# Rolling a matrix by 100 columns: head loads moved from GpSimd's ring to those of SP and ACT, in stages of 256 rows on 64 partitions

## The chip, the core and the metric

The kernel runs on one core of one Trainium2 chip. The metric is the device time of one execution in microseconds (us). The core has 16 DMA engines, which serve several rings (queues): one that the SP engine (SyncE) issues into, one for ACT (ScalarE), and one for POOL (GpSimd), which is a ring written by software. VectorE (DVE) does the only computing, if copying within the on-chip memory (SBUF) may be called that.

## The reference

```python
def setup_inputs():
    return {"x": np.random.randn(8192, 8192).astype(np.float32), "shift": 100}

def reference(x, shift):
    return np.roll(x, shift, axis=1)
```

Every row of 8192 floats (32 KB) is shifted right by 100 places: `out[r, c] = x[r, c - 100]`, and the last 100 floats of a row of x become the first 100 of that row of out. The matrix is 268.44 MB, read once and written once. There is no arithmetic.

## The kernel before

With a shift of s = 100, a is 100 rounded up to a multiple of 128, that is 128, and then made 256 by lines 21 and 22; g = a - s = 156. The output is cut at column a.

**The copies** (lines 34 to 43) write columns 256 to 8191 of out straight from columns 156 to 8091 of x, HBM to HBM. Rows go in 128 blocks of 64. A block is four DMAs (j = 0 to 3) of 16 rows each, four rows apart: 16 pieces of 31,744 bytes, 496 KB. DMAs with j even go to SP, those with j odd to ACT. In the last four blocks each is cut at a middle column into two of 15,872 bytes a row. These are 528 DMAs and 260.08 MB. The framework puts a semaphore wait on a copy, so that SP and ACT issue a new one when an earlier one has landed.

**The heads** (lines 60 to 80) are the first 256 columns of out. They go through SBUF, in 16 stages of 512 rows: 128 partitions with four neighbouring rows (Q = 4) in each. For each stage GpSimd issues three loads:

- line 72 loads t, three pieces of 256 floats (1 KB) per partition: the last 100 floats of one row and the first 156 of the next lie side by side in x, so one piece holds the head of one row and the rest of the head of the next
- line 73 loads into h the 100 floats (400 bytes) that end the fourth row
- line 76 loads into h the 156 floats (624 bytes) that begin the first row

DVE then copies the two parts of t to their places in h (lines 74 and 77). All 16 stages have their own t and h, so no load waits for a buffer. The stores come in a second loop (lines 79 and 80), also on GpSimd: one DMA per stage, which writes 512 pieces of 1 KB to out. GpSimd issues in the order of the program: 48 loads, then 16 stores.

Copies and heads touch different columns of out, and nothing orders them against each other, apart from the engines that they share.

Of the kernel before, what the change touches and what calls it, by code (L numbers as in the profile page):

```python
# [1 line left out]

# [4 lines left out]


@with_exitstack
def kernel(  # L10
    ctx: ExitStack,
    tc: tile.TileContext,
    x: bass.AP,
    shift: int,
    out: bass.AP,
):
    nc = tc.nc
    n_rows, n_cols = x.shape
    s = shift % n_cols
    a = -(-s // 128) * 128  # L20
    if 0 < a <= 384 and a + 128 <= n_cols:
        a += 128
    g = a - s
    P = nc.NUM_PARTITIONS
    engines = [nc.sync, nc.scalar]
    n_chunks = 16
    rows = n_rows // n_chunks

    xm = x.rearrange("(c e j) w -> c j e w", e=16, j=4)
    om = out.rearrange("(c e j) w -> c j e w", e=16, j=4)
    if a < n_cols:
        blocks = n_rows // 64
        mid = (a + n_cols) // 256 * 128
        for c in range(blocks):
            parts = ((a, mid), (mid, n_cols)) if c >= blocks - 4 and a < mid else ((a, n_cols),)  # L40
            for j in range(4):
                for lo, hi in parts:
                    engines[j % 2].dma_start(out=om[c, j, :, lo:hi], in_=xm[c, j, :, lo - s:hi - s])
    if a == 0:
        return


    if a > 512:
        for i in range(n_chunks):
            r = slice(i * rows, (i + 1) * rows)  # L50
            nc.gpsimd.dma_start(out=out[r, :s], in_=x[r, n_cols - s:])
            if g > 0:
                nc.gpsimd.dma_start(out=out[r, s:a], in_=x[r, :g])
        return

    Q = 4  # L60
    n_st = n_rows // (P * Q)
    reads = ctx.enter_context(tc.tile_pool(name="reads", bufs=n_st))
    heads = ctx.enter_context(tc.tile_pool(name="heads", bufs=n_st))
    xt = x.rearrange("(k p q) c -> k p q c", q=Q, p=P)
    ot = out.rearrange("(k p q) c -> k p q c", q=Q, p=P)
    tiles = []
    for k in range(n_st):
        t = reads.tile([P, Q - 1, a], x.dtype)
        h = heads.tile([P, Q, a], x.dtype)
        lead = bass.AP(tensor=x.tensor, offset=(k * P * Q + 1) * n_cols - s,  # L70
                       ap=[[Q * n_cols, P], [n_cols, Q - 1], [1, a]])
        nc.gpsimd.dma_start(out=t[:], in_=lead)  # L72
        nc.gpsimd.dma_start(out=h[:, Q - 1, :s], in_=xt[k, :, Q - 1, n_cols - s:])  # L73
        nc.vector.tensor_copy(h[:, :Q - 1, :s], t[:, :, :s])  # L74
        if g > 0:
            nc.gpsimd.dma_start(out=h[:, 0, s:], in_=xt[k, :, 0, :g])  # L76
            nc.vector.tensor_copy(h[:, 1:, s:], t[:, :, s:])  # L77
        tiles.append(h)
    for k, h in enumerate(tiles):
        nc.gpsimd.dma_start(out=ot[k, :, :, :a], in_=h[:])  # L80


# [1 line left out]
_INS = ['x', 'shift']  # L84
_OUTS = [((8192, 8192), 'float32')]

_NUMBERS = {'shift': 100}


# [26 lines left out]
```

## Time and profile before

| what | value |
|---|---|
| time of the runs, median of 3 | 826.37 us (825.38 to 826.65) |
| span of the profiled execution, first to last instruction | 828.0 us |
| DVE busy | 12.3 us, 32 instructions |
| POOL busy (issuing included) | 41.3 us, 68 instructions |
| copies: time from issue to landing, median | 12.7 us (halves 5.9 to 6.0) |
| stores of heads, issue to landing, median | 108.2 us |
| loads of heads, issue to landing, median | 50.6 us (t), 43.2 and 49.9 us (the two into h) |
| first and last issue of a head load | 1.3 and 241.7 us |
| first and last issue of a head store | 242.2 and 379.6 us |
| chain that ended last | DMA 29% of the span by name, 15% a queue that it can't name |

The profiled execution has no separate time besides its span; the span is 1.6 us above the median of the runs.

The page's slices cut the span into 40 parts of 20.7 us. "DMA" there is the mean busy share of the 16 DMA engines in tenths, "GB/s" what these moved; a copy from HBM to HBM counts its bytes once. A row of a DMA queue has packets, MB, and the time of its packets as a share of 16 engines' span; q1 and q10 are the rings of SP and ACT, q0 is GpSimd's. A window's table does the same for a part of the span. A row of waits has the waiting engine and line, what it waited for, the total in us, how often, and the longest. A row of DMA issues has what was moved, the issuing engine (SPq, ACTq, POOLq), how many, KB each, and the median us from issue to landing.

### The profile page before, as it was taken

What the parts mean: (1) busy time and instruction counts of PE and PEld (TensorE: products, weight loads), DVE (VectorE), ACT (ScalarE), POOL (GpSimd) and SP (SyncE); (2) the same over time, 40 slices, a digit from 0 to 9 for tenths busy, and PEclk for the clock granted to TensorE, in tenths of its full rate; (3) what the DMA queues carried; (4) which work ended last, traced back from release to release, by engine and by line L of the source; (5) the groups of instructions that cost most, each with busy time, mean ns of one, the idle gap of its engine ahead of it and who ended that gap; (6) DMA issues with size and microseconds to landing.
All of it is one profiled execution on the core that took longest, in us unless ns stands there. A gap on an engine that the chain in (4) does not pass through costs nothing. (4 is left out here: it accounts for less than half of the span.)

```text
span 828.0 us, 689 instructions
## 1 busy us (share of the span) xinstructions
DVE 12.3 (1%) x32; POOL 41.3 (5%) x68
## 2 busy tenths in 40 slices
DVE  0000000000010000000000000000000000000000
POOL 2011000000021100000000000000000000000000
DMA  9999999999999999999999999999999999999998
GB/s 308 340 350 334 344 340 337 337 339 344 337 342 348 352 351 345 354 339 346 347 341 344 333 325 325 319 330 333 330 324 322 335 330 328 322 331 328 327 314 300
DMA packets 22278, 276.90 MB, mean 334 GB/s; under 512 B 9473, under 2 KB 9729, under 8 KB 13825
## 3 DMA queue, kind: packets, MB, share of 16 engines
q1 hardware_dynamic: 8448, 130.04, 46.1%
q10 hardware_dynamic: 8448, 130.04, 44.7%
q0 software_dynamic: 5376, 16.78, 8.4%
q14 instruction: 6, 0.04, 0.0%
HBM read 268.44 MB, written 268.44 MB: 648 GB/s over the span
## 5 line engine op out<-in xcount | busy, mean ns | idle before, releaser
L80 POOL DMA_DIRECT2D out_dram<-h x16 | 11.5, 724 | 126.6 <-DMA out_dram<-h 86.8
L76 POOL DMA_DIRECT2D h<-in_x_dram x16 | 8.7, 542 | 141.4 <-DMA t<-in_x_dram 141.4
L72 POOL DMA_DIRECT2D t<-in_x_dram x16 | 12.2, 762 | 30.8 <-DMA h<-in_x_dram 30.0
L73 POOL DMA_DIRECT2D h<-in_x_dram x16 | 8.9, 559 | 39.9 <-DMA h<-in_x_dram 39.9
L74 DVE COPY h<-t 128x300 f32<-128x300 f32 x16 | 6.1, 382 | 260.2 <-DMA t<-in_x_dram 260.2
L77 DVE COPY h<-t 128x468 f32<-128x468 f32 x16 | 7.5, 467 | 0.0
L97 POOL MEMSET const-float32-0.0<- 128x1 f32 x1 | 0.1, 99 | 0.2 <-issue 0.2
L97 POOL MEMSET const-bfloat16-1.0<- 128x1 bf16 x1 | 0.1, 102 | 0.0
L97 POOL MEMSET const-float32-1.0<- 128x1 f32 x1 | 0.1, 99 | 0.0
L97 POOL MEMSET const-uint8-127<- 128x1 uint8 x1 | 0.1, 99 | 0.0
## 6 DMA issues: line engine op xcount, KB each, us to landing
out_dram<-in_x_dram ACTq DMA_DIRECT2D x248, 496.0 KB, 12.7
out_dram<-in_x_dram SPq DMA_DIRECT2D x248, 496.0 KB, 12.7
out_dram<-h POOLq DMA_DIRECT2D x16, 512.0 KB, 108.2
t<-in_x_dram POOLq DMA_DIRECT2D x16, 384.0 KB, 50.6
out_dram<-in_x_dram SPq DMA_DIRECT2D x16, 248.0 KB, 6.0
out_dram<-in_x_dram ACTq DMA_DIRECT2D x16, 248.0 KB, 5.9
h<-in_x_dram POOLq DMA_DIRECT2D x16, 78.0 KB, 43.2
h<-in_x_dram POOLq DMA_DIRECT2D x16, 50.0 KB, 49.9
```

Of the source, the lines that this page charges most:

```text
L72: nc.gpsimd.dma_start(out=t[:], in_=lead)
L73: nc.gpsimd.dma_start(out=h[:, Q - 1, :s], in_=xt[k, :, Q - 1, n_cols - s:])
L74: nc.vector.tensor_copy(h[:, :Q - 1, :s], t[:, :, :s])
L76: nc.gpsimd.dma_start(out=h[:, 0, s:], in_=xt[k, :, 0, :g])
L77: nc.vector.tensor_copy(h[:, 1:, s:], t[:, :, s:])
L80: nc.gpsimd.dma_start(out=ot[k, :, :, :a], in_=h[:])
L97: nc = _bacc.Bacc("TRN2", target_bir_lowering=False, num_devices=1)
```

## The change

The 16 stages of 512 rows on 128 partitions become 32 stages of 256 rows on 64 partitions (H = 64), four rows in each partition as before. The three loads of a stage are issued by SP and ACT: t by the one, the two loads into h by the other, and the roles alternate from stage to stage. They are placed among the copies: after every second block of copies (step = 128 // 64 = 2) comes one stage, so that the stages follow blocks 1, 3, 5, up to 63, and blocks 64 to 127 have none. The buffers are fewer: 4 for t and 12 for h, used in turn. The store of a stage stays with GpSimd, and follows directly on its stage in program order. DVE's copies are the same with half the partitions, 64 of them in place of 32. The copies have the same shapes, order and engines.

```diff
+    blocks = n_rows // 64
+    mid = (a + n_cols) // 256 * 128
+
+    def copies(c):
+
+        last = None
+        parts = ((a, mid), (mid, n_cols)) if c >= blocks - 4 and a < mid else ((a, n_cols),)
+        for j in range(4):
+            for lo, hi in parts:
+                if lo < hi:
+                    last = engines[j % 2].dma_start(out=om[c, j, :, lo:hi], in_=xm[c, j, :, lo - s:hi - s])
+        return last
...
     Q = 4
-    n_st = n_rows // (P * Q)
-    reads = ctx.enter_context(tc.tile_pool(name="reads", bufs=n_st))
-    heads = ctx.enter_context(tc.tile_pool(name="heads", bufs=n_st))
-    xt = x.rearrange("(k p q) c -> k p q c", q=Q, p=P)
-    ot = out.rearrange("(k p q) c -> k p q c", q=Q, p=P)
-    tiles = []
-    for k in range(n_st):
-        t = reads.tile([P, Q - 1, a], x.dtype)
-        h = heads.tile([P, Q, a], x.dtype)
-        lead = bass.AP(tensor=x.tensor, offset=(k * P * Q + 1) * n_cols - s,
-                       ap=[[Q * n_cols, P], [n_cols, Q - 1], [1, a]])
-        nc.gpsimd.dma_start(out=t[:], in_=lead)
-        nc.gpsimd.dma_start(out=h[:, Q - 1, :s], in_=xt[k, :, Q - 1, n_cols - s:])
+    H = P // 2
+    n_st = n_rows // (H * Q)
+    xt = x.rearrange("(k p q) c -> k p q c", q=Q, p=H)
+    ot = out.rearrange("(k p q) c -> k p q c", q=Q, p=H)
+    reads = ctx.enter_context(tc.tile_pool(name="reads", bufs=4))
+    heads = ctx.enter_context(tc.tile_pool(name="heads", bufs=12))
+    step = max(1, blocks // (2 * n_st))
+    for c in range(blocks):
+        copies(c)
+        k, at = divmod(c, step)
+        if at != step - 1 or k >= n_st:
+            continue
+        t = reads.tile([H, Q - 1, a], x.dtype)
+        h = heads.tile([H, Q, a], x.dtype)
+        lead = bass.AP(tensor=x.tensor, offset=(k * H * Q + 1) * n_cols - s,
+                       ap=[[Q * n_cols, H], [n_cols, Q - 1], [1, a]])
+        one, other = engines[k % 2], engines[1 - k % 2]
+        one.dma_start(out=t[:], in_=lead)
+        other.dma_start(out=h[:, Q - 1, :s], in_=xt[k, :, Q - 1, n_cols - s:])
         nc.vector.tensor_copy(h[:, :Q - 1, :s], t[:, :, :s])
         if g > 0:
-            nc.gpsimd.dma_start(out=h[:, 0, s:], in_=xt[k, :, 0, :g])
+            other.dma_start(out=h[:, 0, s:], in_=xt[k, :, 0, :g])
             nc.vector.tensor_copy(h[:, 1:, s:], t[:, :, s:])
-        tiles.append(h)
-    for k, h in enumerate(tiles):
         nc.gpsimd.dma_start(out=ot[k, :, :, :a], in_=h[:])
```

More of the change, by code (lines that the diff above doesn't have):

```diff
@@ L35 @@
     om = out.rearrange("(c e j) w -> c j e w", e=16, j=4)
-    if a < n_cols:
-        blocks = n_rows // 64
-        mid = (a + n_cols) // 256 * 128
-        for c in range(blocks):
[L40 to L49, printed above, removed]
+    blocks = n_rows // 64
[8 more added lines that the diff above has]
+        return last
+    if a == 0 or a > 512:
+        for c in range(blocks):
+            copies(c)
+        for i in range(n_chunks if a else 0):
             r = slice(i * rows, (i + 1) * rows)
@@ L60 @@
     Q = 4
-    n_st = n_rows // (P * Q)
-    reads = ctx.enter_context(tc.tile_pool(name="reads", bufs=n_st))
-    heads = ctx.enter_context(tc.tile_pool(name="heads", bufs=n_st))
-    xt = x.rearrange("(k p q) c -> k p q c", q=Q, p=P)
-    ot = out.rearrange("(k p q) c -> k p q c", q=Q, p=P)
-    tiles = []
-    for k in range(n_st):
-        t = reads.tile([P, Q - 1, a], x.dtype)
-        h = heads.tile([P, Q, a], x.dtype)
-        lead = bass.AP(tensor=x.tensor, offset=(k * P * Q + 1) * n_cols - s,
-                       ap=[[Q * n_cols, P], [n_cols, Q - 1], [1, a]])
-        nc.gpsimd.dma_start(out=t[:], in_=lead)
-        nc.gpsimd.dma_start(out=h[:, Q - 1, :s], in_=xt[k, :, Q - 1, n_cols - s:])
+    H = P // 2
[6 more added lines that the diff above has]
+    for c in range(blocks):
+        copies(c)
+        k, at = divmod(c, step)
[8 more added lines that the diff above has]
+        other.dma_start(out=h[:, Q - 1, :s], in_=xt[k, :, Q - 1, n_cols - s:])
         nc.vector.tensor_copy(h[:, :Q - 1, :s], t[:, :, :s])
         if g > 0:
-            nc.gpsimd.dma_start(out=h[:, 0, s:], in_=xt[k, :, 0, :g])
+            other.dma_start(out=h[:, 0, s:], in_=xt[k, :, 0, :g])
             nc.vector.tensor_copy(h[:, 1:, s:], t[:, :, s:])
-        tiles.append(h)
-    for k, h in enumerate(tiles):
         nc.gpsimd.dma_start(out=ot[k, :, :, :a], in_=h[:])
```

## The prediction

> **What bounds the kernel now.** I read the page's slices and DMA queues first, because the engines hardly compute.
>
> ```profile
> DMA  9999999999999999999999999999999999999998
> GB/s 308 340 350 334 344 340 337 337 339 344 337 342 348 352 351 345 354 339 346 347 341 344 333 325 325 319 330 333 330 324 322 335 330 328 322 331 328 327 314 300
> ...
> q1 hardware_dynamic: 8448, 130.04, 46.1%
> q10 hardware_dynamic: 8448, 130.04, 44.7%
> q0 software_dynamic: 5376, 16.78, 8.4%
> ...
> HBM read 268.44 MB, written 268.44 MB: 648 GB/s over the span
> ```
>
> The 16 DMA engines have no idle slice. q1 and q10 are the rings of SP and ACT with the copies, q0 is GpSimd's ring with the heads. The second half, where heads are gone, runs at a lower GB/s, so the rate has to be read by stage. The same table for three windows follows: 20 to 240 us (copies and head loads), 280 to 460 us (copies and head stores), 500 to 790 us (copies alone); columns are packets, MB, share of the 16 engines.
>
> ```profile
> q10 hardware_dynamic: 2129, 33.88, 42.1%
> q1 hardware_dynamic: 2146, 33.91, 40.2%
> q0 software_dynamic: 2579, 7.04, 17.1%
> ```
>
> ```profile
> q1 hardware_dynamic: 1747, 27.75, 46.8%
> q10 hardware_dynamic: 1746, 27.72, 43.4%
> q0 software_dynamic: 1887, 6.87, 10.6%
> ```
>
> ```profile
> q1 hardware_dynamic: 3001, 47.69, 50.9%
> q10 hardware_dynamic: 2997, 47.46, 48.5%
> ```
>
> A copy reads and writes HBM, so its bytes count twice there; a head load or store counts once. Copies alone: 95.15 MB in 290 us are 328.1 GB/s, 656 in HBM traffic. With loads: copies 67.79 MB in 220 us are 308.1, loads 32.0, together 648. With stores: copies 55.47 MB in 180 us are 308.2, stores 38.2, together 655. The HBM sum is the same within 1.3% in all three, although q0 took 17.1% of the engines' time in one and nothing in another. So HBM traffic sets the pace, and the engines' busy time stretches to fill the span: in the load window a copy ran at 308.1/16/0.823 = 23.4 bytes per ns of engine time, alone at 20.6. The change moves no byte less.
>
> **What the heads cost now.** Loads: 220 x (1 - 308.1/328.1) = 13.4 us for 7.04 MB, so 16.0 us for all 8.39 MB. Stores, the same way: 10.9 us for 6.87 MB, 13.3 us in all. The copies' 260.08 MB at 328.1 GB/s take 792.7 us; the sum is 822.0, and 6.0 us of the 828.0 us span are start and end. The profiled span is 1.6 us above the median of the runs shown (826.37), so I subtract 1.6 at the end.
>
> **Loads on the rings of SP and ACT.** The floor is HBM alone: 8.39 MB at 656 GB/s are 12.8 us, a gain of 3.2 us. The other end of the hidden case is today's 16.0, no gain. Nearest row between: the stores, whose equal bytes cost 13.3. I take the middle, 14.6: **-1.4 us**. This holds only while HBM stays the bound. In engine time the loads took 0.171 x 220 x 16 = 602 us for 7.04 MB in 2579 packets, 11.7 bytes per ns, 233 ns per packet. On q0 pieces of rows are merged: 16 stages of 640 loaded and 512 stored pieces (1 KB or less) are 18,432 pieces, in 5376 packets, landing marks among them. On q1 and q10 a copy has 32 packets for 16 pieces, one per piece and one mark, and no row shows a hardware piece under 15.5 KB. So each stage may now be 20 small packets per engine (12 + 4 + 4), 640 in all. By bytes they cost 8.39 MB/16/11.7 = 45 us per engine, 70 ns a packet, as now; by packets, 640 x 233 = 149 us. Room: the first 64 blocks and all heads take about 130.04 MB/328.1 + 16.0 + 13.3 = 426 us; copies at 23.4 bytes per ns need 347 us of each engine, stores (305 us of engine time for 6.87 MB, 22.5 bytes per ns) 23 us. That leaves 56 us, 87 ns a packet. I take the bytes' price, because the pieces and their sources stay the same; the packets' price goes into the range.
>
> The Trainium skill, "DMA: Bandwidth & Descriptors", speaks against the change: "Rules for kernel authors" wants 128 partitions and at least 1 MiB per DMA, and "Anatomy of one DMA" gives about 2.0 us fixed for each. By that, 48 more transfers would be an estimate of 96 us if none were covered; the trace lets today's 48 land after 43 to 51 us each without such a sum. Its section "Issuing engines are not separate DMA queues" says that another issuer saves only issue time; by that my -1.4 would be 0.
>
> **Fewer copies in flight.** The queue's own waits and the issue rows:
>
> ```profile
> SPq L43 <- DMA out_dram<-in_x_dram: 680.3, 260, 4.9
> ```
>
> ```profile
> out_dram<-in_x_dram ACTq DMA_DIRECT2D x248, 496.0 KB, 12.7
> out_dram<-in_x_dram SPq DMA_DIRECT2D x248, 496.0 KB, 12.7
> out_dram<-h POOLq DMA_DIRECT2D x16, 512.0 KB, 108.2
> ```
>
> SP waits 680 of 828 us for its earlier copies. 528 copies of 12.7 us in 828 us are 8.1 in flight: a copy is issued when the one eight before it has landed. If that limit counts the loads too, 3 of 11 places go to them, so 5.8 copies on average, 5 at worst. The end of the run shows a shallower ring: there the eight in flight are halves (248 KB), worth four copies. The table of windows (length, DVE, POOL, clock, DMA share, GB/s):
>
> ```profile
> 801.00:822.00 21.00, 0.00 (x0) 0.00 (x0) 1.00 0.94 321
> 806.00:824.00 18.00, 0.00 (x0) 0.00 (x0) 1.00 0.96 330
> ...
> 500.00:800.00 300.00, 0.00 (x0) 0.00 (x0) 1.00 0.99 328
> ```
>
> At a depth of four the rate is 2.1% lower or 0.6% higher, by where the window is cut. 5.8 lies 0.55 of the way from eight to four: 0.55 x 426 us x these ends gives +4.9 to -1.4 us. I take the middle, **+1.7 us**.
>
> **Issue and compute, at nothing.** The 96 added issues, 48 on each of SP and ACT, cost 0.51 to 0.86 us each (the copies' shortest and longest rows), 24 to 41 us per engine; SP's 680 us of waiting hide them. Without that cover a copy behind would be late by up to three issues, 2.6 us, less than the 7.7 us that five copies last (508 KB at 328 GB/s are 1.55 us). POOL loses 48 issues (12.2 + 8.9 + 8.7 us) and has 32 stores at up to 0.72 us. DVE's 64 copies at 0.38 to 0.47 us are 24 to 30 us, where 12.3 were, on an engine at 1%.
>
> **New waits.** A load into t waits for DVE's copies four stages back, one into h for the store twelve stages back; behind either stand that ring's copies, and behind those the end. A stage is eight copies and its heads: 426/32 = 13.3 us, so the waits fall due 53 and 160 us later. Stores on q0 were issued one per landing every 13.8 us from 283.4 to 379.6 us (seven steps), 6.9 us for half the size: the ring is half loaded, and its longest landing, eight deep, was 119.3 us. So I cost it at 0. In the other case, each us past 160 is a us on one ring while the other still feeds the engines, so less than that us on the end.
>
> **Sum.** 828.0 - 1.4 + 1.7 = 828.3, less 1.6: **826.7 us**. What the measurement can tell from no change is about 0.2%, 1.65 us: same is 824.7 to 828.0.
>
> **Rivals.**
> *Loads at HBM's price and the depth free: faster.* 828.0 - 3.2 - 1.6 = 823.2, with the depth's good end (-1.4) 821.8. For it: the load window's 648 against 656, and the 330 of one window at a depth of four. Against: a longer line of small packets ahead of copies.
> *The engines become the bound: slower.* Place: the first 426 us, where 20 small packets per stage and engine stand in line with the copies. It decides from 87 ns a packet on; today's price by bytes is 70, by packets 233. At 110 ns: 640 x 110 = 70 us, 14 over the room, 828.3 + 14 - 1.6 = 841. At the geometric middle, 128 ns, 82 us: 853. The far end, 149 us, gives 920. For it: no row shows hardware packets this small. Against: bytes, pieces and sources are those of today.
> *The shallow ring starves the engines: slower.* 4.9 us with loads at 16.0: 828.0 + 4.9 - 1.6 = 831.3. For it: the share 0.94 at the end. Against: the 330 beside it.
> *It doesn't do what it says:* if most of the ring's time went on as before, nothing changes, which is inside the forecast.
>
> **Chances.** Forecast (824.5 to 829.5) 0.45, of it 0.04 faster, 0.21 same, 0.20 slower; HBM price 0.30, faster; engines 0.16 and starving 0.09, slower. So faster 0.34, same 0.21, slower 0.45. The range is 820 to 842: about 0.05 lies below, in gains that no row prices, and 0.1 above, in the engines' case past 110 ns.
>
> **What would show it.** Right: q0 with 8.39 MB of stores alone; HBM sums of 648 to 656 in every window; time to landing of a copy in the first half near 5.8 x 1.6 = 9 us; loads taking near 45 us of engine time; no wait of SP or ACT for a store. Wrong: HBM sums under 640 in the first half, idle shares there, or small packets over 87 ns each. The prediction falls if the first half's HBM rate moves by over 1%, or if the second half's differs at all.

## The result, and the profile after

The changed kernel is slower by half a per cent: 830.93 us median of 13 runs (825.99 to 833.75), where the kernel before had 826.37 us (825.26 to 829.17) beside it. The ratio is 1.005, with a 95% interval of 1.0036 to 1.0064, so 3.0 to 5.3 us were lost. The forecast was 826.7 us in a range of 820 to 842, with slower as the likeliest class at 0.45. So the time lies in the range, but outside the forecast's own band of 824.5 to 829.5.

The profiled execution after spans 828.5 us and took 830.3 us, so 1.8 us lie around the span. The other kernels of this study have 1.7 to 2.0 us there too. If that holds for the profile of the kernel before, its 828.0 us span belongs to an execution of about 829.8 us, 3.4 us above its median. So the two profiles lie only 0.5 us apart where the medians lie 4.6 us apart, and the small loss can't be read off the two spans. It takes pairs of timed runs.

The page's slices and DMA queues after:

```profile
DMA  9999999999999999999999999999999999999998
GB/s 308 341 352 346 340 354 338 331 339 353 334 330 325 363 339 346 351 338 353 329 358 333 326 326 328 334 333 326 326 330 328 320 326 330 323 334 336 328 307 304
...
q1 hardware_dynamic: 14336, 134.24, 48.9%
q10 hardware_dynamic: 14336, 134.24, 47.3%
q0 software_dynamic: 2560, 8.39, 2.5%
...
HBM read 268.44 MB, written 268.44 MB: 648 GB/s over the span
```

The change did what it says: q0 holds the stores' 8.39 MB alone, and q1 and q10 got 4.2 MB each. Their packets went from 8448 to 14,336. Of these 5888, 5120 are pieces of head loads (320 per engine and ring, 640 for both, one packet for every piece), and the rest are landing marks. The engines are as full as before.

The DMA issues of the first 426 us (count, KB each, median us to landing), in which all the loads lie:

```profile
out_dram<-in_x_dram ACTq DMA_DIRECT2D x128, 496.0 KB, 9.3
out_dram<-in_x_dram SPq DMA_DIRECT2D x128, 496.0 KB, 9.1
out_dram<-h POOLq DMA_DIRECT2D x31, 256.0 KB, 9.6
t<-in_x_dram SPq DMA_DIRECT2D x16, 192.0 KB, 12.0
t<-in_x_dram ACTq DMA_DIRECT2D x16, 192.0 KB, 12.4
```

A copy lands after 9.1 to 9.3 us, where the median of the kernel before was 12.7: fewer copies are in flight (256 of some 9.2 us in 426 us are 5.5 on average, where the prediction worked out 8.1 for the kernel before), as they would be if loads hold places among the eight transfers that SP and ACT have under way together. Stores land after 9.6 us, where eight deep they took 108.2. The longest rows of SP's own waits:

```profile
SPq L41 <- DMA out_dram<-in_x_dram: 511.8, 194, 6.2
SPq L73 <- DMA out_dram<-in_x_dram: 63.9, 16, 6.3
SPq L41 <- DMA t<-in_x_dram: 50.7, 16, 5.8
SPq L41 <- DMA h<-in_x_dram: 6.5, 12, 1.1
```

Line 41 is the copy, lines 72, 73 and 76 are the three loads. Loads wait for copies and copies for loads, as places come free. No row of SP names a store, so the buffers of t and h did not hold up its ring. The view has no rows for ACT; that ACT did not wait either is concluded from the stores, which land after 9.6 us, where a buffer of h is needed again only some 160 us later.

### The profile page after: what moved, and what is told of

It is laid out like the page before. It is cut to its first block, busy times and chain, and to the rows that moved or that the text cites. A ratio compares the mean times of both kernels' runs of the same rounds, so it can differ in the third digit from the quotient of the medians.

```text
span 828.5 us, 913 instructions
## 1 busy us (share of the span) xinstructions
DVE 23.8 (3%) x64; POOL 18.9 (2%) x36
## 3 DMA queue, kind: packets, MB, share of 16 engines
q0 software_dynamic: 2560, 8.39, 2.5%
## 4 chain that ended last, share of the span: by engine, by line
DMA 51%; issue 1%; SPq 1%; ACTq 0%; DVE 0%; POOLq 0%; DVEq 0%
DMA out_dram<-in_x_dram 36%; DMA h<-in_x_dram 8%; DMA t<-in_x_dram 7%; SPq L41 1%; ACTq L41 0%; POOLq L109 0%; DVE h L74 0%; DVE h L77 0%; DVEq L74 0%; POOLq L78 0%; SPq L72 0%; SPq L73 0%; ACTq L73 0%
## 5 line engine op out<-in xcount | busy, mean ns | idle before, releaser
L78 POOL DMA_DIRECT2D out_dram<-h x32 | 18.7, 584 | 417.4 <-DVE h L77 417.4
L74 DVE COPY h<-t 64x300 f32<-64x300 f32 x32 | 11.5, 359 | 411.9 <-DMA t<-in_x_dram 354.6
L77 DVE COPY h<-t 64x468 f32<-64x468 f32 x32 | 14.7, 459 | 0.0
## 6 DMA issues: line engine op xcount, KB each, us to landing
t<-in_x_dram ACTq DMA_DIRECT2D x16, 192.0 KB, 12.4
```

## The experiments

Two theories stood at the start. "Depth" says that the loads take places from the copies. "Packets" says that the 20 small packets per engine and stage cost more than HBM's price. A "place" is one of the eight transfers under way together; "HBM's price" is bytes over 656 GB/s, and the "HBM sum" of a window counts the bytes of copies twice and those of heads once. The first four runs take the kernel apart. All times below are medians, beside runs of the kernel before on the same chip (826.7 to 827.2 us). A bracket has the ratio to these and its 95% interval. The ratio is not always that of the two medians, so small steps are also given by it.

### The copies alone

Both pools, the stage's body and its condition are cut from the changed kernel.

```diff
     for c in range(blocks):
         copies(c)
-        k, at = divmod(c, step)
...
-        nc.gpsimd.dma_start(out=ot[k, :, :, :a], in_=h[:])
```

> Leaves out the heads altogether: columns 0 to 255 of out are not written, only the 528 copies run. The window rates priced the heads of the kernel before at 16.0 + 13.3 us, so all theories expect 826.4 - 29.3 = about 797 us. It is the base line for the next three runs. If it is above 805, the heads were hidden more than the windows say; below 790, they cost more.

Measured: 798.89 us (ratio 0.9655, 0.9642 to 0.9668). The heads of the kernel before, 826.89 us beside this run, cost 28.0 us in all, where HBM's price for 16.78 MB at 656 GB/s is 25.6. So it had only some 2.4 us to give.

### Tiny loads in the loads' places

```diff
+        t = reads.tile([16, 3, 16], x.dtype)
         one, other = engines[k % 2], engines[1 - k % 2]
-        one.dma_start(out=t[:], in_=lead)
...
+        one.dma_start(out=t[:, 0], in_=xm[c, 0, :, :16])
+        other.dma_start(out=t[:, 1], in_=xm[c, 1, :, :16])
+        other.dma_start(out=t[:, 2], in_=xm[c, 2, :, :16])
```

> Leaves out the heads as copies_only does, but issues three tiny loads (16 pieces of 64 bytes) on SP and ACT after every second block, at the places where the changed kernel has its head loads. They take the same places in the line of eight DMAs in flight, with hardly any bytes and 3 small packets per engine in place of 20. Theory 'depth' (the loads take 3 of 11 places, so fewer copies are in flight): 3 to 5 us above copies_only, and a rate below 325 GB/s in the first 400 us. Theory 'packets' (the 20 small packets per engine empty the HBM for a moment): within 1 us of copies_only.

Measured: 800.45 us (0.9668, 0.9652 to 0.9683), 1.6 us above the copies alone, with intervals that overlap. That lies between what "packets" (within 1 us) and "depth" (3 to 5 us) had said. DMA issues from 20 to 240 us:

```profile
out_dram<-in_x_dram SPq DMA_DIRECT2D x71, 496.0 KB, 8.3
out_dram<-in_x_dram ACTq DMA_DIRECT2D x70, 496.0 KB, 8.4
t<-in_x_dram ACTq DMA_DIRECT2D x27, 1.0 KB, 9.9
t<-in_x_dram SPq DMA_DIRECT2D x26, 1.0 KB, 9.6
```

A tiny load holds its place for nearly 10 us, about as long as a real one (6.6 to 12.4 us in the changed kernel), presumably because it stands in its ring behind copies. Copies land after 8.3 us, so 141 in 220 us are 5.4 in flight, as few as in the changed kernel, and still only about a third of the loss is seen. The rate did not fall below 325 GB/s, as "depth" asked; it was 327.

### The loads alone, on SP and ACT and on GpSimd

From the changed kernel, and from the kernel before, DVE's copies and the stores are cut.

```diff
-        nc.vector.tensor_copy(h[:, :Q - 1, :s], t[:, :, :s])
...
-            nc.vector.tensor_copy(h[:, 1:, s:], t[:, :, s:])
...
-        nc.gpsimd.dma_start(out=ot[k, :, :, :a], in_=h[:])
```

> Leaves out DVE's copies and the head stores: the copies and the head loads of the changed kernel on SP and ACT, nothing else. Theory 'depth': copies_only + 12.8 (HBM's price of 8.39 MB) + 3 to 5 = about +17 us, and the difference to tiny_loads is 12.8. Theory 'packets': +17 to +21 us too, but the difference to tiny_loads is 16 or more. Theory 'neither' (the loads are as cheap as HBM allows and the loss lies in the stores or their order): +13 us.

> Leaves out DVE's copies and the head stores of the kernel before: its copies and its 48 head loads on GpSimd's ring. The windows priced these loads at 16.0 us, so copies_only + 16. If the change lost its time in the loads, this is 3 to 5 us below loads_hw; if they are equal, the time was lost elsewhere.

Measured: 817.96 us on SP and ACT (0.9888, 0.9874 to 0.9901), 814.56 us on GpSimd (0.9849, 0.9835 to 0.9862). Over the copies alone the loads cost 19.1 us there and 15.7 us here. The gap of 3.4 us (0.39% by the ratios) is most of the change's loss, though intervals of 0.13% on either side leave some 1 to 5.5 us open. The two runs differ in the ring and also in the stage size, 64 against 128 partitions, so the gap can't be put down to the ring alone. The difference to the tiny loads is 17.5 us, where "depth" expected 12.8 and "packets" 16 or more. DVE's copies and the stores add 13.0 us to the one (830.93, from the first pair of runs) and 12.3 to the other (826.89).

The DMA queues from 20 to 240 us (packets, MB, share), first the copies alone, then with loads on SP and ACT, then with loads on GpSimd:

```profile
q10 hardware_dynamic: 2272, 35.88, 50.7%
q1 hardware_dynamic: 2286, 36.26, 49.4%
```

```profile
q1 hardware_dynamic: 5282, 36.64, 49.5%
q10 hardware_dynamic: 5327, 36.87, 49.2%
```

```profile
q1 hardware_dynamic: 2140, 33.97, 40.9%
q10 hardware_dynamic: 2134, 33.88, 39.5%
q0 software_dynamic: 2842, 7.73, 19.3%
```

Alone, copies move 72.14 MB, 656 GB/s of HBM traffic. With loads on SP and ACT, 17 stages of 0.262 MB were issued there, 4.46 MB, so copies had 69.05 MB: 2 x 313.9 + 20.3 = 648 GB/s. With loads on GpSimd it is 2 x 308.4 + 35.1 = 652 GB/s, although these windows hold 1.7 times the loads. So GpSimd's loads, in stages of 128 partitions, lowered the HBM sum less than those on SP and ACT in stages of 64, although they took more engine time.

### Fewer and longer packets

```diff
         lead = bass.AP(tensor=x.tensor, offset=(k * H * Q + 1) * n_cols - s,
-                       ap=[[Q * n_cols, H], [n_cols, Q - 1], [1, a]])
+                       ap=[[Q * n_cols, H], [1, (Q - 1) * a]])
...
-        one.dma_start(out=t[:], in_=lead)
+        one.dma_start(out=t[:].rearrange("p q c -> p (q c)"), in_=lead)
```

> Leaves out DVE's copies and the head stores like loads_hw, and loads t as one piece of 3 KB per partition (768 floats in a row of x, not the three row ends) in place of three of 1 KB. The same three DMAs per stage, places, bytes and order; 12 packets per engine and stage in place of 20. Measured before: copies alone 798.9, with tiny loads 800.45, loads_hw 817.96, loads_sw 814.56. Of loads_hw's 19.1 us, 12.8 are HBM's price and 1.6 the places; 4.7 are left. Theory 'packets' (the number of small packets costs them): 8 of 20 packets less save 1.9 to 4.7, so 813 to 816. Theory 'depth' or 'order': no change, 818.

Measured: 815.24 us (0.9875, 0.9854 to 0.9895) against 817.96 (0.9888, 0.9874 to 0.9901). By the medians the step is 2.7 us, which "packets" expects (1.9 to 4.7), but by the ratios it is 1.1 us, and the intervals overlap, so it shows nothing firm.

### The stage size undone, and halved

```diff
-    H = P // 2
+    H = P
```

> The changed kernel with the stage size undone: 16 stages of 512 rows on 128 partitions, one after every fourth block, loads still on SP and ACT. Loads take 3 of 19 places, the packets are as many, but 40 come in a row. Changed kernel 830.9, before 826.4. Theory 'depth': the places cost half, so about 829 or less. Theory 'packets', each with its own price: 831 as now. Theory 'burst' (the loss grows with the length of the line of small packets, while which little goes over HBM): 833 or more.

> The changed kernel with stages of 128 rows on 32 partitions, one after each of the first 64 blocks, with twice the buffers (8 and 24). 10 small packets per engine in a row, 64 times; loads take 3 of 7 places. Theory 'depth': 4.6 copies in flight, 833 or more. Theory 'packets': 831. Theory 'burst': below 830.

Measured: 828.33 us with 128 partitions (1.0018, 1.0004 to 1.0031), 830.85 us with 32 (1.0048, 1.0033 to 1.0064). With 128 partitions the interval lies apart from that of the changed kernel: some 2.6 us of the loss go with the stage size. "Burst" falls, because the line of small packets was twice as long there, and so does "packets" as a price for each packet, because there were as many (831 expected). "Depth" had asked for about 829 or less, and has it here. But with 32 partitions the time is that of 64, where "depth" asked for 833 or more and "burst" for less than 830. The DMA queues from 20 to 420 us, with 64 partitions (the changed kernel), with 128, and in the kernel before:

```profile
q1 hardware_dynamic: 9345, 64.54, 47.3%
q10 hardware_dynamic: 9348, 64.83, 47.0%
q0 software_dynamic: 2400, 7.87, 4.9%
```

```profile
q1 hardware_dynamic: 9060, 65.02, 47.7%
q10 hardware_dynamic: 8972, 65.14, 47.4%
q0 software_dynamic: 2113, 7.74, 5.2%
```

```profile
q1 hardware_dynamic: 3883, 61.65, 42.5%
q10 hardware_dynamic: 3852, 61.18, 42.2%
q0 software_dynamic: 4732, 14.53, 15.3%
```

The first two have 7.86 MB of loads in q1 and q10 by then (30 stages, or 15 double ones). The copies had 121.5 MB and 122.3 MB. The HBM sums are 647 and 651 GB/s, and 0.6% of 400 us are the 2.4 us between the two profiled executions. The kernel before has 650 GB/s in this window; its profiled execution was one of the longer ones, as said above.

### Crossed rings

With 11 transfers per stage, an odd number, the transfer eight back can be one of the other ring, so that SP would come to wait for ACT's transfers. Four loads in place of three keep the turns.

```diff
+        one, other = engines
+        one.dma_start(out=t[:, :2], in_=lead2)
         other.dma_start(out=h[:, Q - 1, :s], in_=xt[k, :, Q - 1, n_cols - s:])
+        one.dma_start(out=t[:, 2], in_=lead1)
```

> The changed kernel with four loads per stage in place of three: t is cut into a load of two pieces and one of one piece per partition, and they go SP, ACT, SP, ACT in every stage. So 12 transfers per stage keep the alternation, and SP's copy waits for SP's transfer eight before, as in the kernel before, while 4 of 12 places go to loads. Changed kernel 830.9. Theory 'crossed rings' (with 11 transfers per stage one ring waits for the other's transfers and runs dry): 828 or less. Theory 'places': 831 to 833. Theory 'packets' (their number and kind are the same): 831.

Measured: 832.39 us (1.0061, 1.0038 to 1.0083). "Crossed rings" asked for 828 or less; the crossing costs nothing that this run shows. The time lies in the 831 to 833 of "places" (another name for "depth"), but its interval overlaps with that of the changed kernel.

### The same stages, further apart

```diff
-    step = max(1, blocks // (2 * n_st))
+    step = 3
```

The second run has `H = P` and `step = 7`.

> The changed kernel with a stage after every third block in place of every second, so that the 32 stages reach to block 96. The packets are the same in number and length of line; loads take 3 of 15 places. Theory 'places' (the loss grows faster than the share of places taken): 829 or less. Theory 'packets', a fixed price per stage: 831.

> Stages of 512 rows on 128 partitions with loads on SP and ACT as in stage128 (828.3), one after every seventh block in place of every fourth, up to block 112: 3 of 31 places. Theory 'places': 827 or less, level with the kernel before (826.4). Theory 'packets': 828.3 as in stage128. It is also the try at a version that beats both; below 825 it would.

Measured: 831.57 us (1.0052, 1.0036 to 1.0068) and 828.64 us (1.0018, 1.0006 to 1.0031), each as its closer-set partner (830.93 and 828.33). "Places" had asked for 829 or less and 827 or less. So the loss doesn't depend, as far as these runs can tell, on how close the stages stand, or on the share of places that the loads hold. It looks like a fixed sum, about 4 us for stages on 64 partitions and 1.5 us for those on 128. None of the tries beats the kernel before.

### Bigger copies

```diff
-        for j in range(4):
+        for j in range(2):
             for lo, hi in parts:
                 if lo < hi:
-                    last = engines[j % 2].dma_start(out=om[c, j, :, lo:hi], in_=xm[c, j, :, lo - s:hi - s])
+                    last = engines[j].dma_start(out=om2[c, :, 2 * j:2 * j + 2, lo:hi], in_=xm2[c, :, 2 * j:2 * j + 2, lo - s:hi - s])
```

The views om2 and xm2 have the order c e j w; the control makes the same edit in the kernel before.

> The changed kernel with copies of 32 rows in place of 16 (two DMAs per block, one on SP and one on ACT, two pieces of 31.7 KB per engine), so that loads take 3 of 7 places but those left hold twice the bytes: 4.6 copies of 992 KB in flight, more than the 8 of 496 KB. Theory 'depth': the loss goes, 827 or less. Theory 'packets' or 'burst': 830 to 832.

> The kernel before with copies of 32 rows (two DMAs per block), the control of big_after (835.3). If the bigger copies are slow by themselves, 830 or more, and big_after tells nothing of the places; if it is 826, big_after's 9 us are the loads' among bigger copies, and 'places' can't be their cause, because more bytes are in flight there.

Measured: 835.29 us (1.0117, 1.0087 to 1.0147) for the changed kernel and 832.6 us (1.007, 1.0047 to 1.0094) for the one before. "Depth" expected 827 or less for the first, "packets" and "burst" 830 to 832. The bigger copies are slow by themselves: from 450 to 770 us, where copies run alone, the changed kernel moves 326 GB/s with them and 328 without. Between the two lie 0.5% again, with intervals that overlap slightly, although a lack of copies in flight can hardly be the reason with twice the bytes in each (120 copies of 15.3 us in 400 us are 4.6 of 992 KB).

## Why the prediction was right or wrong

**What bounds the kernel: right.** The copies alone ran in 798.9 us where the window rates gave 797. From 20 to 420 us the HBM sum was 647 GB/s after the change and 650 before it, within the 1% that the prediction allowed though 1 GB/s under its sign of 648, and 656 to 657 where copies run alone, before and after. By the trace's packet records the loads took 28.3 us of each engine, where near 45 was the sign. With nothing but loads beside the copies they took 37.6 us on SP and ACT and 46.4 on GpSimd: the engine time that was freed bought nothing.

**The price of the loads: this step failed.** "I take the middle, 14.6: -1.4 us" held that loads on SP and ACT would cost between HBM's price and today's. They cost 19.1 us, above today's 15.7: the term was +3.4, not -1.4, and the bounds that I gave the hidden case left out a loss. The floor was sound, the ceiling was not. "No worse than now" was no row of the trace. The only loss I allowed for loads was the engines as the bound, and that is not how it came. Nor had the smaller stage a term of its own in the sum: some 2.6 us came back with 128 partitions, more than half of the loss. What is left to the move onto SP and ACT, with its new order of loads and stores, is about 1.5 us.

**Fewer copies in flight: the mechanism seen, the price not confirmed.** The loads do count against the eight, and copies landed after 9.1 to 9.3 us where 9 was expected. The +1.7 us was met by 1.6 in the tiny loads, inside their uncertainty. But spreading the stages out won nothing back, and with 32 partitions, where copies landed after 7.7 to 8.0 us, nothing more was lost, so the loss hardly comes from places. The rival of a shallow ring gave 831.3, next to the 830.93 measured. That is chance, for its mechanism is this one.

**The engines as the bound: fell.** It was to decide from 87 ns a packet on. The 640 packets per engine took 28.3 us, 44 ns each, and 1 KB took 46 ns in the median. The upper part of the range, which holds the result, stood there for this case and the shallow ring's, so it is luck that the time lies in the range.

**Issue, compute and new waits at nothing: right.** SP still waits over 600 us, none of its waits names a store (ACT's waits have no rows), and DVE is busy 23.8 us.

**Where the time starts from: right.** 828.0 less 1.6 is 826.4, the median before. From there the sum forecast +0.3 us, and +4.6 were measured. But the window rates were read from an execution that was probably some 3.4 us above the median, so the prices taken from them can be off by a few us in all.

**The Trainium skill.** "DMA: Bandwidth & Descriptors", "Rules for kernel authors", asks for 128 partitions. The runs agree in sign: 128 partitions were 2.6 us better than 64. It also asks for at least 1 MiB per DMA. No run here has DMAs of that size; on the way there, the kernel before was 0.7% slower with copies of 992 KB than with copies of 496 KB. The 2.0 us of "Anatomy of one DMA" stand there for GpSimd's path, and the 48 added loads are on SP and ACT, so the prediction's 96 us stretched them; 96 loads more, with 32 partitions, cost nothing that the runs show. "Issuing engines are not separate DMA queues" lets another issuer save issue time alone, and that there was nothing to gain agrees. That there was something to lose, about 1.5 us with the stage size undone, it doesn't say.

**What stays open:** why stages on 64 or 32 partitions cost some 2.6 us more than on 128, and why the move costs about 1.5 us even with 128. Partitions, pieces per transfer, the number of loads, and the size and number of stores change together there. Against a price per load speaks that 192 loads cost no more than 96. That the loss comes with fewer than 128 partitions fits all six runs, but it was not tried by itself. Engines that idle now and then are another candidate: the shares of the queues from 20 to 420 us add up to 99.2% with 64 partitions and 100.3% with 128 (records of packets overlap a little), and 1.1% of 400 us are 4.4 us. But with 32 partitions they add up to 97.3%, and the time is that of 64, so idle engines by themselves don't explain it. Also open is whether the small packets' length matters; the run for it was within its uncertainty.

## What to carry to other kernels

When every DMA engine is busy all the time, add up the HBM traffic by stage first, counting HBM to HBM copies twice. If the sum stays nearly the same while the kinds of work change, as here, expect little from engine time saved. Cutting the kernel to its copies showed within one run that some 2.4 us were to be had in all. For a bound on a moved transfer, "as now" is not a ceiling: leave room for a loss that is as large as the gain. And when a change alters two things, here the ring and the stage size, give each a term and a run of its own.

## What was not expected

- Beside the copies alone, loads on GpSimd's software ring in stages of 128 partitions took more time to land (41 to 48 us against 6.6 to 11.0) and more engine time (46.4 us against 37.6 per engine) than loads on SP and ACT in stages of 64, and yet cost 3.4 us less of the kernel's time. How much of that is the ring's was not tried.
- Copies of 992 KB in two pieces per engine were slower than copies of 496 KB in one, 832.6 us against 827.2.
- Small packets on the rings of SP and ACT were cheap in engine time in the changed kernel: 24 ns for 400 bytes, 32 for 624, 46 for 1 KB in the median, 44 ns a packet on average.
